# Stick-breaking attention summed by parts over differences of the values, with scans that take two keys a step in long rows

## The chip, the core and the metric

The kernel runs on one core of a Trainium2 chip. The metric is the device time of one execution in microseconds, lower is better. Engines are named as in the profile: PE is TensorE's matmul, PEld its weight load, DVE VectorE, ACT ScalarE, POOL GpSimd, SP SyncE. Each engine works through its own list of instructions in order, and waits where an instruction needs another engine or a transfer.

## The reference

One step of a two-layer streaming encoder: 1024 prompt frames and 8 sample streams of 16 frames, width 1024. Layer 0 has eight stick-breaking heads of width 64 beside a convolution; layer 1 is a band attention; each layer ends with an MLP of width 4096. The change lies in the stick-breaking heads:

```python
def stick_breaking(q, k, v, q_pos, k_pos):
    z = jnp.einsum('bqhd,bkhd->bhqk', q, k).astype(jnp.float32) * (HEAD_DIM ** -0.5)
    mask = k_pos[None, :] < q_pos[:, None]
    log_keep = jnp.where(mask, jax.nn.log_sigmoid(-z), 0.0)
    between = lax.cumsum(log_keep, axis=3, reverse=True) - log_keep
    w = jnp.where(mask, jnp.exp(jax.nn.log_sigmoid(z) + between), 0.0)
    return jnp.einsum('bhqk,bkhd->bqhd', w.astype(v.dtype), v)
```

With keep_j = sigmoid(-z_j), and 1 for a masked key, and S_j the product of keep over the keys from j to the row's end, the weight of key j is sigmoid(z_j) S_{j+1}, which equals S_{j+1} - S_j.

## The kernel before, in words

Everything is kept transposed, with channels on the 128 partitions and tokens along the free axis. The heads of layer 0 are worked on in four pairs p = 0 to 3, in `mixer0`. While a pair's attention runs, other work is laid between its steps: the q, k and v projections of the next pair (`proj`, tiles `sq`, `sk`, `sv`, PSUM tiles `psp`), the two gated inputs of the convolution (`ag`, tiles `u`), the 31 taps of the convolution (`tap`, line 735, two DVE instructions each, tiles `y`), the sample streams (`sample_steps`), and in the last pair the layer norm of the convolution (`conv_norm`) and the first part of the output projection (`part_out`, tiles `psoa`, which read `cat`, loaded through `cr` by `ready_chunks`).

`attend` makes eight jobs a pair: head i = 0 or 1, and t = 0 to 3, two rows of queries each. A row q is 128 queries against n = (q + 1) * 128 keys, so n runs from 128 to 1024. `one(q)` makes the scores in banks of up to 512 keys (lines 924, 925, 927, tile `z`; the last adds a mask of -1e30 on the block of the diagonal). ACT takes sigmoid(z) into `w` (tile `sg`, line 928) and sigmoid(-z) into `keep` (tile `kp`, line 929). `stick` lets DVE turn `keep` into running products from the row's end (a scan along the free axis, line 907: it steps backward through the row, its second input is a constant 1) and multiplies `w` by the product of the keys behind it (line 909). The sample streams do the same with one row of 1152 keys for each of two groups of four streams (`soft`, tiles `sgs` and `kps`).

`weigh_steps` then transposes the weights in blocks of 128 by 128 on PE (`turn`, line 388, PSUM tile `tpa`), copies them to SBUF on ACT (line 390, `wa`), and multiplies them with the values (`prod`, line 398, tile `ava`: two halves of the PSUM bank hold two partial sums). `finish` copies one half with ACT (line 406), adds the halves on DVE (line 410, `cpa`) and stores them. Values reach that product through `expand_v`: PE transposes `sv` in blocks (line 898, `vt`), ACT copies them into `vs` (line 900).

The order of the work is written with numbers: `merge` puts the lists of steps together by their estimated PE times and by lags behind named steps, `level` lays the taps between them by estimated DVE times, and the framework's own scheduler then fixes the order of each engine's list from the dependences. `tap` is recorded after the last DVE instruction of `finish`. Tiles of one tag share buffers: three for `sg`, two for `kp`, one for `sv`.

The pair's `sv` is also an output: POOL issues its store (line 881) when all three parts have been evacuated.

Of the kernel before, what the change touches and what calls it, by code (L numbers as in the profile page):

```python
# [124 lines left out]
def tile_trunk(ctx, tc, ins, outs):  # L125
# [17 lines left out]
    def bank(name):  # L143
        return psum.tile([P, 512], F32, tag="ps", name=name)
# [225 lines left out]
                split(hi, lo, piece[rows, at - c0:at - c0 + m])  # L370
                at += m

    def weigh_steps(vs, wk, cat, i, t, blocks, name, scored):


        order = sorted(blocks.keys, key=lambda j: -len(blocks.keys[j]))
        groups = []
        for two in zip(order[::2], order[1::2]):
            n, m = (P * len(blocks.keys[j]) for j in two)
            groups.append(([(two[0], 0, n), (two[1], n, m)], n + m))  # L380
        st = {"w": {}}

        def turn(gi):
            items, used = groups[gi]
            tp = bank(f"tp{name}{gi}")
            for j, c0, n in items:
                for q, tile_q in enumerate(blocks.keys[j]):
                    nc.tensor.transpose(tp[:, c0 + q * P:c0 + (q + 1) * P], blocks.get(j, tile_q), ident)
            st["w"][gi] = wk.tile([P, 512], F32, tag="wt", name=f"w{name}{gi}")
            ACT(st["w"][gi][:, :used], tp[:, :used], AF.Copy)  # L390

        def prod(gi):

            if gi == 0:
                st["av"] = bank(f"av{name}")
            for m, (j, c0, n) in enumerate(groups[gi][0]):
                o0 = 0 if 2 * t in blocks.keys[j] else P
                mm(st["av"][64 * m:64 * m + 64, o0:o0 + n], vs[:, j, i], st["w"][gi][:, c0:c0 + n], start=gi == 0,
                   stop=gi == last)

        def finish():
            own = slice(64 * i, 64 * i + 64)
            av = st["av"]
            one = P if t == 0 else 0
            tmp = wk.tile([P, 256], F32, tag="av", name=f"at{name}")
            ACT(tmp[own, one:], av[64:128, one:256], AF.Copy)
# [3 lines left out]
            prior["weights"] = tt(piece[own, one:], av[0:64, one:256], tmp[own, one:], ALU.add)  # L410
# [244 lines left out]
    def mixer0():  # L655
        with ExitStack() as st:
# [8 lines left out]
            pp = Bufs(st.enter_context(pool("pair0")))  # L665
            wk = Bufs(st.enter_context(pool("work0")), wt=4, wts=1, cat=2)
            S = {"qb": qb}

# [216 lines left out]
            def expand_qk(p):  # L885
# [19 lines left out]
            def stick(w, keep, n):  # L905

                nc.vector.tensor_tensor_scan(keep[:, 0:n][:, ::-1], keep[:, 0:n][:, ::-1],  # L907
                                             ones[:, 0:1].to_broadcast([P, n]), 1.0, ALU.mult, ALU.mult)
                tt(w[:, 0:n - 1], w[:, 0:n - 1], keep[:, 1:n], ALU.mult)

            def attend(p, cat):
                def job(i, t):
                    ws = {}

                    def one(q):
                        n = (q + 1) * P
                        w = ep.tile([P, TP], F32, "sg", f"sg{p}{i}{q}")
                        keep = ep.tile([P, TP + P], F32, "kp", f"kp{p}{i}{q}")
                        qc = slice(q * P, q * P + P)
                        for c in range(0, n, 512):  # L920
                            m = min(512, n - c)
# [3 lines left out]
                            mm(z[:, :m], qs[i][:, qc], kl[i][:, c:c + m], start=False, stop=not last)  # L925
                            if last:
                                mm(z[:, m - P:m], unit, maskd, start=False, stop=True)
                            ACT(w[:, c:c + m], z[:, :m], AF.Sigmoid)
                            ACT(keep[:, c:c + m], z[:, :m], AF.Sigmoid, scale=-1.0)
                        stick(w, keep, n)  # L930
                        ws[q] = w
# [8 lines left out]
                    def dcost(q):  # L940
# [2 lines left out]
                    name = f"a{p}{i}{t}"  # L943
                    return (Step(cost(q0), lambda: one(q0), dcost(q0)),
                            Step(cost(q1), lambda: one(q1), dcost(q1), f"z{name}"),
                            weigh_steps(vs, wk, cat, i, t, blocks, name, f"z{name}"))

                return [job(i, t) for i in range(2) for t in range(4)]

            def soft(bg, z, zn, s):  # L950
# [1016 lines left out]
```

## Time and profile before

| what | us |
|---|---|
| median of 3 runs (lowest, highest) | 2755.19 (2753.42, 2755.53) |
| span of the profiled execution, first to last instruction | 2748.2 |
| what the median has beyond that span | 7.0 |
| busy: PE, DVE, ACT, POOL | 2669.0, 2090.5, 1389.0, 328.3 |
| mean granted TensorE clock | 0.991 |

The profiled execution's own time is its span; only the 7.0 us between it and the median of the runs are not seen in the trace. In the profile, "idle before" is the time in which an engine stood still before an instruction, and what is named behind an arrow is what ended it. A matmul's busy time overlaps with the next one's, so a busy PE needn't be PE at its peak. PEclk is the granted share of TensorE's clock. Times in a row of the timeline are the start, counted from the span's first instruction, and the length of a run of like instructions.

### The profile page before, as it was taken

What the parts mean: (1) busy time and instruction counts of PE and PEld (TensorE: products, weight loads), DVE (VectorE), ACT (ScalarE), POOL (GpSimd) and SP (SyncE); (2) the same over time, 40 slices, a digit from 0 to 9 for tenths busy, and PEclk for the clock granted to TensorE, in tenths of its full rate; (3) what the DMA queues carried; (4) which work ended last, traced back from release to release, by engine and by line L of the source; (5) the groups of instructions that cost most, each with busy time, mean ns of one, the idle gap of its engine ahead of it and who ended that gap; (6) DMA issues with size and microseconds to landing.
All of it is one profiled execution on the core that took longest, in us unless ns stands there. A gap on an engine that the chain in (4) does not pass through costs nothing.

```text
span 2748.2 us, 50583 instructions
## 1 busy us (share of the span) xinstructions
PE 2669.0 (97%) x19362; PEld 2557.1 (93%) x19362; DVE 2090.5 (76%) x4117; ACT 1389.0 (51%) x2906; POOL 328.3 (12%) x599
## 2 busy tenths in 40 slices
PE   8999898999999999999999999998999999999998
PEld 8987776799999999999999999997999999999998
DVE  8999998888777755758577777778787777647577
ACT  5344456755554543435355555556555555434344
POOL 1100101041111100000011111110221111100001
PEclk9999999999999999999999999999999999999999
DMA  4434446454343377435444444446533343684344
GB/s 157 121 111 147 118 141 223 145 176 143 139 146 141 138 260 250 124 100 170 146 140 138 140 135 135 139 132 229 179 132 137 141 145 138 230 270 134 96 125 145
DMA packets 173203, 422.90 MB, mean 154 GB/s; under 512 B 25968, under 2 KB 53808, under 8 KB 170912
## 3 DMA queue, kind: packets, MB, share of 16 engines
q1 hardware_dynamic: 135696, 288.38, 33.1%
q0 software_dynamic: 37120, 131.27, 13.9%
q8 instruction: 152, 2.49, 0.4%
q14 instruction: 91, 0.75, 0.1%
q10 hardware_dynamic: 144, 0.02, 0.0%
HBM read 289.60 MB, written 117.34 MB: 148 GB/s over the span
## 4 chain that ended last, share of the span: by engine, by line
PE 76%; DVE 12%; ACT 4%; issue 4%; DMA 3%; POOL 0%; SPq 0%; DVEq 0%; ACTq 0%; POOLq 0%
PE um L1461 25%; PE pd L1686 25%; PE psc L225 10%; PE psp L225 3%; DVE y L735 3%; PE avc L467 2%; PE tpc L455 2%; DVE kp L907 2%; PE f L225 1%; PE psoa L225 1%; DMA cr<-cat_d 1%; PE zc L1201 1%; PE zc L1202 1%; PE zs L568 1%; PE so L602 1%
## 5 line engine op out<-in xcount | busy, mean ns | idle before, releaser
L225 PE MATMUL psc<-h,hl_wc 128*128 128x384 f32 x1728 | 327.2, 339 | 0.0
L225 PEld LDWEIGHTS psc<-h,hl_wc 128*128 128x128 f32 x1728 | 296.8, 188 | 13.3 <-issue 10.9
L1461 PE MATMUL um<-sl,hl_m 128*128 128x288 f32 x1548 | 240.3, 295 | 0.0
L1461 PEld LDWEIGHTS um<-sl,hl_m 128*128 128x128 f32 x1548 | 217.7, 188 | 0.0
L1686 PE MATMUL pd<-tm,hl_wd 128*128 128x288 f32 x1584 | 214.7, 294 | 0.0
L1686 PEld LDWEIGHTS pd<-tm,hl_wd 128*128 128x128 f32 x1584 | 211.3, 189 | 0.0
L735 DVE SCALAR_TENSOR_TENSOR y<-u,dw,y 128x1024 f32<-128x1024 f32 (+1 forms) x232 | 177.8, 806 | 0.6
L225 PE MATMUL psp<-h,hl_wi 128*128 128x384 f32 x864 | 165.7, 344 | 0.0
L1468 ACT ACTIVATE hdm<-hdm 128x288 f32<-128x288 f32 x192 | 84.7, 442 | 156.5 <-DVE hdm L1467 154.8
L225 PEld LDWEIGHTS psp<-h,hl_wi 128*128 128x128 f32 x864 | 150.9, 191 | 7.0 <-issue 6.2
L186 DVE TENSOR_TENSOR tm<-xr,tm 128x576 fp32r<-128x576 f32 (+1 forms) x120 | 85.8, 715 | 93.9 <-ACT tm L185 93.6
L185 ACT ACTIVATE tm<-xr 128x576 fp32r<-128x576 f32 (+1 forms) x120 | 77.6, 646 | 95.8 <-PE pd L1686 74.0
L1168 ACT ACTIVATE s<-s,mxc 128x640 f32<-128x640 f32 (+4 forms) x128 | 88.9, 694 | 60.2 <-DVE mxc L1165 58.6
L1461 PE MATMUL um<-sl,hl 128*128 128x288 f32 x756 | 119.1, 296 | 0.0
L1686 PE MATMUL pd<-th,hl_wd 128*128 128x288 f32 x792 | 113.7, 297 | 3.8 <-DVE th L186 3.7
L1686 PEld LDWEIGHTS pd<-th,hl_wd 128*128 128x128 f32 x792 | 108.2, 190 | 4.8 <-DVE th L186 4.2
L1686 PE MATMUL pd<-xr,hl_wd 128*128 128x288 f32 x792 | 112.4, 296 | 0.0
L1686 PEld LDWEIGHTS pd<-xr,hl_wd 128*128 128x128 f32 x792 | 108.0, 190 | 0.0
L1461 PEld LDWEIGHTS um<-sl,hl 128*128 128x128 f32 x756 | 106.4, 188 | 0.8
L1686 PE MATMUL pd<-tm,hl 128*128 128x288 f32 x768 | 104.9, 295 | 0.0
L1686 PEld LDWEIGHTS pd<-tm,hl 128*128 128x128 f32 x768 | 103.1, 188 | 0.0
L185 ACT ACTIVATE whc<-tpc 128x512 fp32r<-128x512 f32 (+1 forms) x144 | 72.5, 523 | 46.7 <-PE tpc L455 45.8
(526 smaller groups left out, 6637.0 us busy)
## 6 DMA issues: line engine op xcount, KB each, us to landing
xr<-hb_d SPq DMA_DIRECT2D x208, 288.0 KB, 3.0
xr<-in_w_up_dram SPq DMA_DIRECT2D x64, 512.0 KB, 4.2
hb_d<-hdm POOLq DMA_DIRECT2D x96, 288.0 KB, 2.4
hb_d<-t POOLq DMA_DIRECT2D x96, 288.0 KB, 2.4
wm<-in_w_down_dram SPq DMA_DIRECT2D x64, 256.0 KB, 4.0
st_wd<-in_w_down_dram SPq DMA_DIRECT2D x64, 256.0 KB, 3.5
st_wc<-in_w_in_c_dram SPq DMA_DIRECT2D x44, 256.0 KB, 2.9
xm_d<-xo POOLq DMA_DIRECT2D x16, 576.0 KB, 3.5
```

The source lines that it names most:

```text
L185: ACT(hi, src, AF.Copy)
L186: return tt(lo, src, f(hi), ALU.subtract)
L225: mm(ps()[:, :G], hl[:, a, at:at + P], act[g][k // 4][b][:, k % 4, :], start=n == 0, stop=n == len(todo) - 1)
L455: nc.tensor.transpose(tp[:, c0 + q * P:c0 + (q + 1) * P], blocks.get(j, tile_q), ident)
L467: mm(st["av"][:, o0:o0 + n], vs[:, j, i].rearrange("p a d -> p (a d)"), src[:, c0:c0 + n], start=st["done"] == 0, stop=st["done"] == nmm - 1)
L568: mm(box["z"][at // 512][own, at % 512:at % 512 + kw], qb[:, own], k[:, b * kw:b * kw + kw], start=True, stop=True)
L735: stt(src if j == CW - 1 else dst, src, wj, dst, ALU.mult, ALU.add)
L907: nc.vector.tensor_tensor_scan(keep[:, 0:n][:, ::-1], keep[:, 0:n][:, ::-1], ones[:, 0:1].to_broadcast([P, n]), 1.0, ALU.mult, ALU.mult)
L1168: ACT(s[:, :n], s[:, :n], AF.Exp, bias=mx, scale=-1.0, accum_out=tot)
L1461: mm(banks[b, n][:, :TQ], w[:, a, c * P:c * P + P], combo(key, c)[:, h, n * TQ:n * TQ + TQ], start=k < 3 and c == 0 and i == 0, stop=c == ...
L1468: ACT(y, y, AF.Relu)
L1686: mm(ps, w[:, a, m * P:m * P + P], b[:, h, (n - ns[0]) * TQ:(n - ns[0]) * TQ + TQ], start=first and s == 0, stop=j == NJ - 1 and s == 2, s ...
```

## The change

Summed by parts, the sum over a row's n keys of (S_{j+1} - S_j) v_j is v_{n-1} plus the sum over j of S_j (v_{j-1} - v_j), with v_{-1} = 0. So the product on PE can take the running products S as they are, if the values are replaced by differences of neighbours, and if the last value of the row's end is added to each output column.

- `one(q)` no longer makes sigmoid(z) (line 928 before) and no longer multiplies by it (line 909 before). One tile, with the tag `sg`, holds `keep` and then S.
- `stick` scans rows under 512 keys as before. In rows of 512 keys and more the scan steps over pairs: it reads the odd keys and the even keys, multiplies both into the running product, and writes S at the even keys (n/2 steps, each input and the output with a step of two elements). A product of n/2 - 1 elements, again with a step of two, makes the odd keys' S.
- `differences(p)`, new, runs ahead of a pair's first transposes of values: four ACT copies of 64 x 8 take the value at the end of each block of 128 keys into `ve`; one DVE subtraction of 128 x 1023 turns `sv` into differences in place, stepping backward; one ACT instruction of 128 x 1 negates the first column. The subtraction overwrites `sv`, so it waits for the store of `sv`; the transposes wait for it.
- `finish` adds the row ends: instead of one ACT copy of 64 x 256 there are two ACT instructions of 64 x 128, each with its own column of `ve` as bias. Where t = 0 there were two instructions before, and are two now.
- `soft` keeps both sigmoids and the product of 1151 elements; its scan of 1152 becomes a scan of 576 and a product of 575.

```diff
@@ finish
-            ACT(tmp[own, one:], av[64:128, one:256], AF.Copy)
...
-            if one:
-                ACT(piece[own, :one], av[0:64, :one], AF.Copy)
+            for e in range(2):
+                cols = slice(e * P, e * P + P)
+                dst, rows = (piece, slice(0, 64)) if one and e == 0 else (tmp, slice(64, 128))
+                ACT(dst[own, cols], av[rows, cols], AF.Identity, bias=ends()[rows, i, 2 * t + e:2 * t + e + 1])
@@ mixer0
+            def differences(p):
+                v = S["sv", p]
+                ends = S["ends", p] = pp.tile([P, 2, 8], F32, "ve", f"ve{p}")
+                for i in range(2):
+                    for rows in (slice(0, 64), slice(64, 128)):
+                        ACT(ends[rows, i], v[64 * i:64 * i + 64, P - 1:TP:P], AF.Copy)
+                tt(v[:, 1:TP][:, ::-1], v[:, 0:TP - 1][:, ::-1], v[:, 1:TP][:, ::-1], ALU.subtract)
+                ACT(v[:, 0:1], v[:, 0:1], AF.Copy, scale=-1.0)
@@ expand_v
+                if g == 0:
+                    differences(p)
@@ stick
-                nc.vector.tensor_tensor_scan(keep[:, 0:n][:, ::-1], keep[:, 0:n][:, ::-1],
-                                             ones[:, 0:1].to_broadcast([P, n]), 1.0, ALU.mult, ALU.mult)
-                tt(w[:, 0:n - 1], w[:, 0:n - 1], keep[:, 1:n], ALU.mult)
+                if n < 512:
+                    nc.vector.tensor_tensor_scan(keep[:, 0:n][:, ::-1], keep[:, 0:n][:, ::-1],
+                                                 ones[:, 0:1].to_broadcast([P, n]), 1.0, ALU.mult, ALU.mult)
+                    return
+                even, odd = keep[:, 0:n:2], keep[:, 1:n:2]
+                nc.vector.tensor_tensor_scan(even[:, ::-1], odd[:, ::-1], even[:, ::-1], 1.0, ALU.mult, ALU.mult)
+                tt(odd[:, :n // 2 - 1], odd[:, :n // 2 - 1], even[:, 1:], ALU.mult)
@@ one(q)
-                        w = ep.tile([P, TP], F32, "sg", f"sg{p}{i}{q}")
-                        keep = ep.tile([P, TP + P], F32, "kp", f"kp{p}{i}{q}")
+                        keep = ep.tile([P, TP], F32, "sg", f"sg{p}{i}{q}")
...
-                            ACT(w[:, c:c + m], z[:, :m], AF.Sigmoid)
                             ACT(keep[:, c:c + m], z[:, :m], AF.Sigmoid, scale=-1.0)
@@ soft
-                stick(w, keep, TP + P)
+                stick(keep, TP + P)
+                tt(w[:, 0:TP + P - 1], w[:, 0:TP + P - 1], keep[:, 1:TP + P], ALU.mult)
```

Where the lists of instructions differ matters at three places. In the rows below, a name's number tells its tile, and a scan is listed as SCALAR_TENSOR_TENSOR; line numbers of the changed kernel are up to 19 higher.

The first is PE's list at the start of pair 0, where the transposes of the values (`vt`, from `sv`) stand among the projections of pair 1 (`psp`); `z` are scores, `zs` a sample stream's scores. Before, they stand in the middle of a projection of 24 matmuls:

```order
L225 MATMUL psp_1108<-h_31_172,hl_wi_0_966 128x384
L225 MATMUL psp_1108<-h_30_171,hl_wi_0_966 128x384
L898 MATMUL vt_1121<-ident,sv_1003 128x128 x3
L898 MATMUL vt_1128<-ident,sv_1003 128x128 x3
L898 MATMUL vt_1133<-ident,sv_1003 128x128 x3
L568 MATMUL zs_1140<-ct00k_1142,qb_124 32x256 x4
L225 MATMUL psp_1108<-h_40_178,hl_wi_1_971 128x384
```

Now they stand behind the whole of it:

```order
L225 MATMUL psp_1105<-h_71_191,hl_wi_1_971 128x384
L225 MATMUL psp_1105<-h_70_190,hl_wi_1_971 128x384
L913 MATMUL vt_1125<-ident,sv_1003 128x128 x3
L913 MATMUL vt_1132<-ident,sv_1003 128x128 x3
L913 MATMUL vt_1137<-ident,sv_1003 128x128 x3
L570 MATMUL zs_1144<-ct00k_1146,qb_124 32x256 x4
L943 MATMUL z_1173<-k_743,q_741 128x256
```

The transposes moved back by twelve matmuls; what they wait for on DVE is new.

The second is DVE's list at the same time. `y` and `u` are taps, `hl_wi` are weights split for PE, `sq` is an evacuation. Before:

```order
L186 TENSOR_TENSOR hl_wi_1_1093<-st_wi_1_1091,hl_wi_1_1093 128x512
L907 SCALAR_TENSOR_TENSOR kp_1099<-kp_1099,ones 128x128
L735 SCALAR_TENSOR_TENSOR y_771<-u_382,dw,y_771 128x1024
L909 TENSOR_TENSOR sg_1098<-sg_1098,kp_1099 128x127
L735 SCALAR_TENSOR_TENSOR y_771<-u_382,dw,y_771 128x1024
L735 SCALAR_TENSOR_TENSOR y_771<-u_382,dw,y_771 128x128
```

Now:

```order
L186 TENSOR_TENSOR hl_wi_1_1093<-st_wi_1_1091,hl_wi_1_1093 128x512
L923 SCALAR_TENSOR_TENSOR sg_1098<-sg_1098,ones 128x128
L737 SCALAR_TENSOR_TENSOR y_771<-u_382,dw,y_771 128x1024
L737 SCALAR_TENSOR_TENSOR y_771<-u_382,dw,y_771 128x128
L737 SCALAR_TENSOR_TENSOR y_771<-u_382,dw,y_771 128x1024
L903 TENSOR_TENSOR sv_1003<-sv_1003 128x1023
```

The subtraction came in behind three taps, and the product of 127 left.

The third is DVE's list where the last row of pair 0 ends (head 1), at its row of 1024 keys; `l` and `q` (lines 351, 353) prepare the next pair's keys and queries. Before:

```order
L877 TENSOR_TENSOR sv_2101<-psp_2110,rh_315 128x384
L735 SCALAR_TENSOR_TENSOR y_1239<-u_389,dw,y_1239 128x128
L735 SCALAR_TENSOR_TENSOR u_389<-u_389,dw,y_1239 128x1024
L735 SCALAR_TENSOR_TENSOR u_389<-u_389,dw,y_1239 128x8x16
L351 TENSOR_TENSOR l_745<-sk_1870,k_743 64x1024
L907 SCALAR_TENSOR_TENSOR kp_2126<-kp_2126,ones 128x1024
L351 TENSOR_TENSOR l_746<-sk_1870,k_744 64x1024
L909 TENSOR_TENSOR sg_2125<-sg_2125,kp_2126 128x1023
```

Now:

```order
L879 TENSOR_TENSOR sv_2071<-psp_2080,rh_315 128x384
L737 SCALAR_TENSOR_TENSOR y_1237<-u_389,dw,y_1237 128x128
L737 SCALAR_TENSOR_TENSOR u_389<-u_389,dw,y_1237 128x1024
L928 SCALAR_TENSOR_TENSOR sg_2095<-sg_2095 128x512
L737 SCALAR_TENSOR_TENSOR u_389<-u_389,dw,y_1237 128x8x16
L929 TENSOR_TENSOR sg_2095<-sg_2095 128x511
L351 TENSOR_TENSOR l_746<-sk_1848,k_744 64x1024
```

The scan and its product now stand ahead of the preparation of the next pair.

More of the change, by code (lines that the diff above doesn't have):

```diff
@@ L371, in put, with weigh_steps @@
                 at += m
-    def weigh_steps(vs, wk, cat, i, t, blocks, name, scored):
+    def weigh_steps(vs, ends, wk, cat, i, t, blocks, name, scored):
         order = sorted(blocks.keys, key=lambda j: -len(blocks.keys[j]))
@@ L903, in expand_v, with stick @@
                     ACT(S["vn"], tp[:, 2 * P:3 * P], AF.Copy)
-            def stick(w, keep, n):
-                nc.vector.tensor_tensor_scan(keep[:, 0:n][:, ::-1], keep[:, 0:n][:, ::-1],
-                                             ones[:, 0:1].to_broadcast([P, n]), 1.0, ALU.mult, ALU.mult)
-                tt(w[:, 0:n - 1], w[:, 0:n - 1], keep[:, 1:n], ALU.mult)
+            def stick(keep, n):
+                if n < 512:
[5 more added lines that the diff above has]
+                tt(odd[:, :n // 2 - 1], odd[:, :n // 2 - 1], even[:, 1:], ALU.mult)
             def attend(p, cat):
@@ L927, in one @@
                                 mm(z[:, m - P:m], unit, maskd, start=False, stop=True)
-                            ACT(w[:, c:c + m], z[:, :m], AF.Sigmoid)
                             ACT(keep[:, c:c + m], z[:, :m], AF.Sigmoid, scale=-1.0)
-                        stick(w, keep, n)
-                        ws[q] = w
+                        stick(keep, n)
+                        ws[q] = keep
                     keys = {j: [q for q in (2 * t, 2 * t + 1) if j <= q] for j in range(2 * t + 2)}
@@ L945, in job @@
                             Step(cost(q1), lambda: one(q1), dcost(q1), f"z{name}"),
-                            weigh_steps(vs, wk, cat, i, t, blocks, name, f"z{name}"))
+                            weigh_steps(vs, lambda: S["ends", p], wk, cat, i, t, blocks, name, f"z{name}"))
                 return [job(i, t) for i in range(2) for t in range(4)]
```

2 lines of the change are left out of this document (1 added, 1 removed).

## The prediction

> **What bounds the kernel now.** I read the page first, for the whole.
>
> ```profile
> span 2748.2 us, 50583 instructions
> PE 2669.0 (97%) x19362; PEld 2557.1 (93%) x19362; DVE 2090.5 (76%) x4117; ACT 1389.0 (51%) x2906; POOL 328.3 (12%) x599
> ```
>
> PE is busy nearly all the time, so a change on DVE or ACT can only bring back time in which PE stands still. The changed instructions lie between 105 us (first scores) and 547 us (last addition of halves), so the second view is the busy time by windows of that stage (PE, PEld, DVE, ACT, POOL, each with its count; then PEclk and DMA).
>
> ```profile
> 105.00:205.00 100.00, 97.86 (x721) 85.55 (x723) 97.67 (x131) 49.65 (x116) 8.47 (x15) 1.00 0.43 128
> ...
> 315.00:415.00 100.00, 93.24 (x717) 77.76 (x716) 98.68 (x127) 53.31 (x127) 10.61 (x19) 0.98 0.48 148
> 415.00:547.00 132.00, 117.61 (x853) 92.38 (x852) 112.06 (x201) 98.59 (x213) 16.07 (x29) 0.96 0.57 190
> sum 442.00, PE 408.35 PEld 340.74 DVE 414.21 ACT 249.84 POOL 44.66; mean PE 102.09 PEld 85.19 DVE 103.55 ACT 62.46 POOL 11.17
> ```
>
> Unlike in the whole kernel, DVE is here as full as PE: 414.2 of 442 us, 98 to 99% in the first window and the third. PE stands still for 442 - 408.35 = 33.7 us, the most that waits alone can give back. PE's list of waits in the same window says on whom (total, times, longest).
>
> ```profile
> PE tpa L388 <- DVE sg L909: 20.2, 8, 6.2
> PE psoa L225 <- ACT cat L185: 5.0, 3, 2.6
> PE sn L582 <- DVE cpa L410: 1.2, 1, 1.2
> ...
> PE tpa L388 <- DVE xo L1086: 0.4, 1, 0.4
> ```
>
> The transposes of the weights wait 20.2 us for the product that the change removes; seven smaller waits for DVE, the first and last of which are shown, make 5.5 us more. The rest is ACT's. The longest wait, at the end of pair 0, shows how it arises.
>
> ```profile
> 206.02 4.44 PE L225 MATMUL psp<-h,hl_wi 128*128 128x384 f32 x24
> ...
> 211.15 0.54 DVE L877 TENSOR_TENSOR sv<-psp,rh 128x384 f32<-128x384 f32 x1
> 211.62 0.33 DVE L735 SCALAR_TENSOR_TENSOR y<-u,dw,y 128x128 f32<-128x128 f32 x1
> 211.88 1.53 DVE L735 SCALAR_TENSOR_TENSOR u<-u,dw,y 128x1024 f32<-128x1024 f32 x2
> 213.34 1.21 DVE L351 TENSOR_TENSOR l<-sk,k 64x1024 fp32r<-64x1024 f32 x1
> 214.47 2.27 DVE L907 TENSOR_TENSOR_SCAN kp<-kp,ones 128x1024 f32<-128x1024 f32 x1
> 218.03 1.23 DVE L909 TENSOR_TENSOR sg<-sg,kp 128x1023 f32<-128x1023 f32 x1
> 211.94 0.33 PE L388 MATMUL tpa<-ident,sg 128*128 128x128 f32 x1
> 219.31 0.90 PE L388 MATMUL tpa<-ident,sg 128*128 128x128 f32 x3 [6.17 <-DVE sg L909]
> ```
>
> DVE works through its list without a gap and is simply late: a backlog, not a missing input.
>
> **The change part by part.** DVE first. These rows give its costs (busy, mean ns).
>
> ```profile
> L907 DVE TENSOR_TENSOR_SCAN kp<-kp,ones 128x1024 f32<-128x1024 f32 x8 | 18.3, 2284 | 0.2
> L907 DVE TENSOR_TENSOR_SCAN kp<-kp,ones 128x128 f32<-128x128 f32 x8 | 3.3, 412 | 0.0
> L909 DVE TENSOR_TENSOR sg<-sg,kp 128x127 f32<-128x127 f32 (+3 forms) x64 | 47.9, 749 | 0.6
> L909 DVE TENSOR_TENSOR sg<-sg,kp 128x1023 f32<-128x1023 f32 x8 | 9.8, 1219 | 0.2
> L909 DVE TENSOR_TENSOR sg<-sg,kp 128x127 f32<-128x127 f32 x8 | 2.2, 280 | 0.0
> ```
>
> A scan of m steps costs 145 + 2.09 m ns by its first two rows, a product 145 + 1.05 m by its last two. Eight heads have rows of 512, 640, 768, 896 and 1024 keys, 3840 in all. Removed: their scans, 8 x (5 x 145 + 2.09 x 3840) = 70.0 us; all products by sigmoid(z), 47.9; the samples' scans of 1152, 8 x 2.55 = 20.4; together 138.3. Added: scans of half the steps, 8 x (725 + 2.09 x 1920) = 37.9; products for the odd keys, 8 x (725 + 1.05 x 1915) = 21.9; for the samples 8 x (1.35 + 0.75) = 16.8; four subtractions of 1023 at 1.22, 4.9; together 81.5. DVE loses 57 us of 414, 14 a pair.
>
> No row shows DVE with a step of two elements. Two bounds: as a step of one (the numbers above), or twice the time per element, since a scan already needs twice a product's (2.09 against 1.05). A gain is excluded, as each element still has to be processed. Doubling the products alone adds 8 x (1.05 x 1915 + 1.05 x 575) = 20.9 us, doubling the scans too another 8 x (2.09 x 1920 + 2.09 x 576) = 41.7. I take the step of one, the row of the same instruction on the same type, and keep both others as rivals.
>
> ACT loses line 928 and gains little:
>
> ```profile
> L928 ACT ACTIVATE sg<-z 128x512 f32<-128x512 f32 (+2 forms) x96 | 47.8, 498 | 19.8 <-PE z L927 10.1 <-PE tpa L388 4.6 <-PE z L925 4.1
> L406 ACT ACTIVATE ata<-ava 64x128 f32<-64x128 f32 x8 | 2.2, 274 | 8.5 <-PE ava L398 8.4
> ```
>
> Its twenty small instructions for `ve` and the first column are at most 274 ns each, 5.5 us, and 24 split copies add under 274 each, 6.6: net 36 us less on an engine at 57% here. Costed at nothing, but it helps: each row's scan can start one sigmoid earlier.
>
> What it brings. With 14 us less a pair, DVE's 97.7 us in the first window become 84, below PE's 97.9: the backlog goes and PE sets the pace. At 219.31 the wait is then set by the inputs. `sv` is ready when its matmuls end, the first twelve of the 24 at 206.02, so about 208.3; behind it stand the tap rows, 0.33 + 1.2, the scan of 512, 1.2, the small tap, 0.3, and the product, 0.7: done by 212.6, where PE comes at 212.05. So 0.5 of 6.2 stays. The next longest (4.1, below) stands at the end of pair 2 and shrinks the same way; for the six others I leave 1.0 in all. Gain 20.2 - 1.5 = 18.7. Of the other 5.5 I take half, 2.7, since those instructions also wait for PE.
>
> TensorE's clock adds to it:
>
> ```profile
> 306.79 0.97 PE L388 MATMUL tpa<-ident,sg 128*128 128x128 f32 x6 [1.64 <-DVE sg L909]
> ...
> 215.20:222.00 6.80, 2.69 (x10) 2.69 (x11) 6.63 (x9) 0.60 (x1) 2.91 (x7) 0.50 0.84 212
> 307.40:310.80 3.40, 3.40 (x40) 2.70 (x38) 3.34 (x5) 0.92 (x2) 0.53 (x1) 0.50 0.19 25
> 406.40:409.80 3.40, 3.40 (x13) 3.30 (x12) 3.34 (x5) 2.21 (x6) 0.54 (x1) 0.50 0.12 31
> ...
> sum 23.80, PE 16.86 PEld 14.05 DVE 19.18 ACT 10.60 POOL 8.15; mean PE 3.37 PEld 2.81 DVE 3.84 ACT 2.12 POOL 1.63
> ```
>
> The last row sums five stretches in which the granted clock was 0.50. The three shown lie at or just behind waits for line 909, as the row above shows for the second; PE worked 2.69 + 3.40 + 3.40 = 9.5 us in them, and would do it in half. Gain 4.7.
>
> What it costs. At the start of pair 0 the transposes of values now wait for a subtraction.
>
> ```profile
> 106.27 2.34 PE L225 MATMUL psp<-h,hl_wi 128*128 128x384 f32 x12
> 106.97 0.56 POOL L881 DMA_DIRECT2D out_sb_v_dram<-sv  x1 [3.93 <-ACT sv L879]
> DMA to landing us min/median/max: 4.0/4.0/4.0
> 109.32 1.25 DVE L735 SCALAR_TENSOR_TENSOR y<-u,dw,y 128x1024 f32<-128x1024 f32 x1
> ```
>
> The store lands at 106.97 + 4.0 = 111.0. On DVE the taps from 109.32 take 1.25 + 0.3 + 1.25, so the subtraction runs from 112.1 to 113.3, not held by the store; ACT's one column, 0.3, ends at 113.6. PE has 24 matmuls from 106.27, twice some 2.2 us, and is there at 110.6: a new wait of 3.0 us. Without the twelve matmuls that moved ahead it would be 5.2. Queued behind ACT's column are the copies of `vs` and the next row's sigmoids, which wait for PE anyway. In pairs 1 to 3 `sv` is made in the pair before, so that store and subtraction have time; I take ACT's one column, 0.3 each, 0.9. A half-clock stretch of 3.4 us behind the new wait costs 1.7, at even odds 0.9. The Trainium skill (TensorE: Matmul & The Clock Gate, What's actually happening) puts the half clock behind an idle window of about 3.4 us; here it also followed a wait of 1.64 us, at 307.4, so I don't count the 3.0 as safe.
>
> At the end of pair 2 a part of the gain comes back:
>
> ```profile
> 419.08 1.05 ACT L348 ACTIVATE k<-sk 64x1024 fp32r<-64x1024 f32 x1 [0.17 <-PE z L924]
> ...
> 424.81 0.34 SPq L1062 DMA_DIRECT2D cr<-cat_d  x1
> 429.67 1.03 PE L388 MATMUL tpa<-ident,sg 128*128 128x128 f32 x6 [4.14 <-DVE sg L909]
> 432.69 1.35 ACT L185 ACTIVATE cat<-cr 128x384 fp32r<-128x384 f32 x3 [1.84 <-DMA cr<-cat_d]
> 433.27 0.69 PE L225 MATMUL psoa<-cat,hl_wo0a 128*128 128x384 f32 x1 [2.57 <-ACT cat L185]
> ```
>
> The load of `cr` starts when DVE has read `sk` (line 351), and lands 7.9 us later. DVE's line 351 waits for ACT's copy of k, at 419.08 + 1.05, and takes 1.2, so the load can start at 421.4, 3.4 us sooner: of 4.1 us 0.8 turn into a wait for `cat`.
>
> Sum: -18.7 - 2.7 - 4.7 + 3.0 + 0.9 + 0.9 + 0.8 = -20.5. Span 2727.7, and with the 7.0 us around it 2734.7.
>
> **The rivals.** A measurement of this kernel tells 0.2%, 5.5 us, from no change.
>
> Strided products cost double. The Trainium skill speaks for it (Vector Engine (DVE) Microarchitecture Reference, Measured stream behaviour on trn2): a port keeps its full rate only on runs of at least two adjacent 4-byte words, and a two-source operation whose elements stand apart took 1.73 to 2.51 ns a column instead of 1.05. Against it the same skill (Advanced Engine Details and Errata, SBUF Cachelines) asks for two hits on a 16-byte line, which a step of 8 bytes has. No run here shows either. DVE then saves 57 - 21 = 36 us and stays at 378 of 442. I take half of the waits and of the clock: 10.1 + 1.4 + 2.4 - 5.6 = 8.3 gained, 2747. Chance 0.22.
>
> The waits change owner. PE's list already has ACT and a load behind DVE; if the ends of pairs stay bound by loads and by ACT's order, only the six short waits go, 20.2 - 6.2 - 4.1 = 9.9, less the 5.6 of costs: 2751, no change that can be told. For it speaks the row at 433.27, against it that ACT is half idle. Chance 0.10.
>
> Slower: scans and products both double. DVE gets 20.9 + 41.7 - 57 = 6 us more, in a stage where it is at 96 to 99% and PE already waits for it; with the 3.0, 0.9 and 0.9 of new costs the time is 2755.2 + 11 = 2766. It decides from the point where an element at a step of two costs about 1.9 times as much in both. Against it: a scan spends 2.09 ns on an element, in which a slower port could hide. Chance 0.08.
>
> **How the numbers follow.** The forecast has 0.60. All DVE waits and half of the 16.9 us of busy PE in half-clock stretches gone, at 2 us of cost, would be about 2723; the rivals of 2747 and 2751 set the upper end at 2752. Faster: 0.60 x 0.98 + 0.22 x 0.9 + 0.10 x 0.2 = 0.81. Slower 0.08, the rest 0.11.
>
> **What would show it.** Right: DVE near 357 us busy over the stage, scans of 512 at 1.2 us and products of 511 at 0.7, waits of `tpa` under 5 us, one wait of some 3 us of `vt` for ACT or DVE in pair 0. Wrong: products of 511 near 1.3 us (first rival), long new waits of PE for `cat`, `vs` or loads (second), scans of 512 near 2.3 us (third), or a stage still 440 us long with DVE at 80%, which would mean that PE's own rate sets it.

## The result and the profile after

| kernel | median, us | runs | lowest to highest |
|---|---|---|---|
| before, same session | 2754.3 | 4 | 2749.0 to 2755.5 |
| changed | 2729.8 | 4 | 2726.0 to 2730.9 |

The ratio is 0.9914, 95% interval 0.9900 to 0.9928: about 24 us less. The forecast was 2734.7 us. The changed kernel was timed once more in a later set: 2728.6 us, ratio 0.9912 (0.9894 to 0.9930).

The page's first lines, for the whole kernel:

```profile
span 2728.9 us, 50505 instructions
PE 2662.6 (98%) x19362; PEld 2553.8 (94%) x19362; DVE 2040.6 (75%) x4105; ACT 1365.7 (50%) x2854; POOL 330.5 (12%) x599
```

The matmuls are the same 19362. DVE has lost 50 us, and the span is 19.3 us shorter than before's 2748.2. The windows of the stage, as in the prediction (PE, PEld, DVE, ACT, POOL with counts, then PEclk and DMA); by the count of matmuls the stage now ends at 527 instead of 547 us:

```profile
205.00:315.00 110.00, 109.99 (x823) 95.56 (x822) 103.90 (x156) 48.84 (x117) 13.22 (x22) 1.00 0.45 140
...
415.00:527.00 112.00, 105.51 (x763) 83.00 (x762) 85.05 (x180) 82.47 (x178) 9.06 (x17) 0.98 0.56 189
sum 422.00, PE 404.49 PEld 340.07 DVE 365.66 ACT 228.10 POOL 45.37; mean PE 101.12 PEld 85.02 DVE 91.41 ACT 57.02 POOL 11.34
```

The row to look at is the first: PE is busy 109.99 of 110 us there, at full clock. In that window PE alone sets the pace. Over the stage it stands still for 422 - 404.49 = 17.5 us, against 33.7 before. PE's waits in the same window:

```profile
PE psoa L225 <- ACT cat L185: 8.0, 3, 5.7
PE vt L913 <- ACT sv L904: 2.9, 1, 2.9
PE tpa L388 <- DVE sg L929: 2.2, 2, 1.3
PE zs L570 <- ACT qb L561: 1.3, 1, 1.3
...
```

The 20.2 us behind line 909 have become 2.2 us behind line 929, two short waits. The other waits for DVE shrank from 5.5 to about 1.4 us. Two owners are new or bigger: `cat` (5.0 before, 8.0 now) and `vt` (none before, 2.9 now). The place that had the longest wait before, the end of pair 0, now reads:

```profile
210.48 0.55 PE L388 MATMUL tpa<-ident,sg 128*128 128x128 f32 x3
210.78 4.42 PE L225 MATMUL psp<-h,hl_wi 128*128 128x384 f32 x24
211.21 0.55 DVE L879 TENSOR_TENSOR sv<-psp,rh 128x384 f32<-128x384 f32 x1
...
213.13 1.21 DVE L928 TENSOR_TENSOR_SCAN sg<-sg 128x512 f32<-128x512 f32 x1
214.27 0.32 DVE L737 SCALAR_TENSOR_TENSOR u<-u,dw,y 128x128 f32<-128x128 f32 x1
214.51 0.68 DVE L929 TENSOR_TENSOR sg<-sg 128x511 f32<-128x511 f32 x1
...
216.67 0.66 PE L388 MATMUL tpa<-ident,sg 128*128 128x128 f32 x4
```

The product of the last row ends at 215.19 and the 24 matmuls at 215.20. PE comes to the row's transposes at 216.67, behind a few other matmuls: DVE is done 1.5 us ahead of it, and 6.2 us of waiting are 0. The durations by form, of the instructions that the change adds:

```profile
L928 DVE TENSOR_TENSOR_SCAN sg<-sg 128x512 f32<-128x512 f32 x8 | 9.7, 1217 | 2.1 <-ACT sg L947 2.0
L929 DVE TENSOR_TENSOR sg<-sg 128x511 f32<-128x511 f32 x8 | 5.5, 691 | 0.2
L928 DVE TENSOR_TENSOR_SCAN sg<-sg 128x256 f32<-128x256 f32 x8 | 5.4, 678 | 1.0 <-ACT sg L947 1.0
L923 DVE TENSOR_TENSOR_SCAN sg<-sg,ones 128x256 f32<-128x256 f32 x8 | 5.5, 684 | 4.4 <-ACT sg L947 4.4
L411 ACT ACTIVATE ata<-ava,ve 64x128 f32<-64x128 f32 x56 | 17.8, 358 | 27.9 <-PE ava L398 27.5
```

Row two answers the first rival, which had 1.3 us for a product of 511: it takes 691 ns. The scans answer the third, which had 2.3 us for a scan of 512: it takes 1217 ns, and a scan of 256 steps takes 678 ns with a step of two words (line 928) and 684 ns with a step of one (line 923). The step of two costs nothing.

### The profile page after: what moved, and what is told of

Read it like the earlier page. It is cut to its first block, busy times and chain, and to the rows that moved or that the text cites. A ratio compares the mean times of both kernels' runs of the same rounds, so it can differ in the third digit from the quotient of the medians.

```text
span 2728.9 us, 50505 instructions
## 1 busy us (share of the span) xinstructions
PE 2662.6 (98%) x19362; PEld 2553.8 (94%) x19362; DVE 2040.6 (75%) x4105; ACT 1365.7 (50%) x2854; POOL 330.5 (12%) x599
## 4 chain that ended last, share of the span: by engine, by line
PE 84%; DVE 7%; ACT 3%; issue 3%; DMA 3%; POOL 0%; SPq 0%; DVEq 0%; ACTq 0%; POOLq 0%
PE pd L1705 26%; PE um L1480 25%; PE psc L225 10%; PE psp L225 4%; PE avc L469 2%; PE tpc L457 2%; PE psoa L225 2%; PE f L225 1%; PE zs L570 1%; PE zc L1220 1%; PE ava L398 1%; DVE y L737 1%; PE so L604 1%; PE psg L225 1%; PE psa L225 1%
```

## The experiments

The theory: DVE's backlog in the stage is what PE waited for, and taking 57 us from DVE brings the gain. Its rivals: the gain is ACT's, which has lost half of its sigmoids; or it is the latency of the longest rows' scans alone. Ratios are to the kernel before, run on the same chip in the same set.

### DVE's load put back

```diff
                         stick(keep, n)
+                        extra = ep.tile([P, TP + P], F32, "kp", f"kp{p}{i}{q}")
+                        tt(extra[:, 0:n - 1], keep[:, 0:n - 1], keep[:, 1:n], ALU.mult)
```

> The changed kernel, and behind each row's scan one more product of n-1 elements into a spare tile that nobody reads: 64 products, in the mean 575 elements, 145 + 1.05 x 575 = 749 ns each by the prediction's own line, 48 us in all, which puts VectorE's stage back from 366 to about 414 us, where it was before (414). ScalarE keeps its saving. Theory (the gain comes from VectorE's backlog, which TensorE's transposes of the weights wait for): the waits of tpa for sg return, though not in full, since a useless product delays only what is behind it in VectorE's queue and a row's own transposes may start ahead of it; 12 to 20 us of tpa waits in the stage, 2742 to 2752 us. Rival (the gain comes from ScalarE's 47 us fewer sigmoids, or from the shorter scan alone, VectorE's load being beside the point): tpa waits below 6 us, at most 2734 us.

2746.0 us, ratio 0.9980 (0.9970 to 0.9990). The added products take 47.8 us (64 of 747 ns in the mean), and 18 of the 24 us are gone. The stage is 440 us long again, with DVE at 402.7 (414 were expected: 47.8 us is a sum of rows, and busy time counts what overlaps once). PE stands still for 440 - 406.91 = 33.1 us of it, as long as before the change (33.7). Its windows, the second one around the longest new wait, and PE's waits:

```profile
104.00:544.00 440.00, 406.91 (x3006) 340.78 (x3006) 402.67 (x653) 228.00 (x520) 44.89 (x80) 0.97 0.48 150
222.00:236.00 14.00, 8.08 (x50) 6.46 (x49) 13.94 (x21) 3.16 (x8) 0.54 (x1) 0.76 0.40 130
```

```profile
PE vt L913 <- ACT sv L904: 10.5, 3, 5.9
PE psoa L225 <- ACT cat L185: 9.2, 2, 5.8
PE tpa L388 <- DVE sg L929: 7.0, 4, 3.3
```

The time is as the theory had it, the place isn't: I had expected 12 to 20 us at `tpa`, and only 7.0 stand there (2.2 without the added products). More, 10.5 us in three waits (2.9 without them), stands at `vt`, so in pairs 1 and 2 too. Their subtraction queues behind DVE's backlog like any other instruction:

```profile
230.96 1.20 DVE L903 TENSOR_TENSOR sv<-sv 128x1023 f32<-128x1023 f32 x1
232.19 0.20 ACT L904 ACTIVATE sv<-sv 128x1 f32<-128x1 f32 x1 [4.51 <-DVE sv L903]
232.45 0.90 PE L913 MATMUL vt<-ident,sv 128*128 128x128 f32 x3 [5.92 <-ACT sv L904]
```

DVE is busy 13.94 of 14 us around it, and PE waits 5.92 us. ACT's saving was untouched in this kernel, and so was each row's own scan: the load alone, placed behind the row, takes three quarters of the gain back.

### ACT's load put back

```diff
+                            ACT(extra[:, c:c + m], z[:, :m], AF.Sigmoid)
                             ACT(keep[:, c:c + m], z[:, :m], AF.Sigmoid, scale=-1.0)
```

> The changed kernel, and ahead of each bank's sigmoid of -z a useless sigmoid of z into a spare tile, as the kernel before had it for the weights: ScalarE's stage goes from 228 to about 275 us, VectorE's stays at 366. Theory (VectorE's backlog): ScalarE has room, each row's scan starts up to 0.75 us later but VectorE is behind at most of these places, so 2730 to 2735 us. Rival (the gain is ScalarE's): most of the 24 us goes, 2745 us or more.

2735.0 us, ratio 0.9940 (0.9926 to 0.9955). ACT is back at 265 us over the stage, and seven tenths of the gain stay. By ratio it is 0.26 to 0.28% slower than the changed kernel, some 7 us, but its interval touches those of the two sets of the changed kernel (0.9928 and 0.9930 at their upper ends), so its size is uncertain. No wait accounts for it: PE stands still for 17.0 us between 100 and 530 us, against 17.5 and 15.4 in the two profiles of the changed kernel. The clock would: the half-clock stretches of the stage sum to 27.3 us, against 13.6 and 17.1. PE worked 20.9 us in them, against 9.8 and 12.1, and half of that difference is 4.4 to 5.5 us. So a minor part, three tenths at most, is ACT's. Even that isn't shown: these are single executions, and where the half-clock stretches fall changes from one to the next (below).

### One part of the change alone

Parts only: every scan of the pairs, the sample streams' too, takes one key a step.

```diff
-                if n < 512:
+                if n < 4096:
```

> The changed kernel with one key a step in every scan of the four pairs, so only the summing by parts is left of the change: a row of 1024 keys costs one scan of 145 + 2.09 x 1024 = 2.29 us in place of 1.22 + 0.69 = 1.91, and of 512 keys 1.22 in place of 0.68 + 0.41; VectorE's stage gets about 14 us more than the 366 of the changed kernel. Theory (the gain goes by VectorE's load; 48 of its 62 us come from the product that the parts do away with): three quarters or more of the gain stays, 2731 to 2737 us. Rival (it goes by the latency of the long scans, which the transposes of the longest rows wait for): half the gain or more goes, 2742 us or more.

2730.6 us, ratio 0.9928 (0.9914 to 0.9943), just under the 2731 to 2737 us that I had expected.

Two keys a step only: the kernel before, with `stick` of the changed kernel ahead of its product by `w`.

> The kernel before with only the two-key scans of long rows; the weights are still made by a sigmoid and a product. VectorE's stage falls by about 14 us from 414 to 400. Theory (load): about 14 of 62 parts of the gain, 2746 to 2752 us, tpa waits of the 20 us down to 12 to 17. Rival (latency of the long scans): half the gain or more, 2742 us or less.

2740.0 us, ratio 0.9964 (0.9951 to 0.9977). I had expected 2746 to 2752 us; the time is the rival's, 2742 or less. Of PE's waits at `tpa`, this row is left of the 20.2 us:

```profile
PE tpa L388 <- DVE sg L914: 13.8, 8, 4.2
```

By ratios the parts alone bring 0.72%, the two keys alone 0.36%, both 0.86%. The two parts add up to 0.22% more than the whole, which is no more than these intervals leave open (some 0.24%). PE's idle time shows it more clearly, in one execution each: between its 500th matmul and its 3560th, PE stands still for 33.8 us before, 21.8 with the two keys alone, 18.7 with the parts alone, and 17.5 and 15.4 in two profiles of both. So the gain saturates: the first 14 us taken from DVE bring 12 us of PE's idle time, the last 14 bring 1 to 3. I had split the gain in proportion to the load, 14 of 62; that was wrong. The rival was nearer with its number, but its reason, the latency of the long scans, doesn't hold: the parts alone leave those scans at one key a step and keep five sixths of the gain. While PE waits at the end of a pair, most of what is taken off the backlog is won; the 20.2 us at `tpa` fell by 6.4, the longest of 6.2 us to 4.2. When DVE has caught up, more brings little.

### The step of two, measured by itself

The changed kernel, with three rounds of instructions of 144 elements behind its start that nobody reads: products at steps of 1, 2, 3, 4, 6, 8 words (lines 988 to 993) and scans at steps of 1, 2, 4, 8 (lines 994 to 997).

```diff
+            def stepped(s):
+                return probe[:, 0:M * s:s]
+            for _ in range(3):
+                tt(stepped(1), stepped(1), stepped(1), ALU.mult)
...
+                nc.vector.tensor_tensor_scan(stepped(8), stepped(8), stepped(8), 1.0, ALU.mult, ALU.mult)
```

> The changed kernel, and behind its start three rounds of products and scans of 144 elements that nobody reads, with steps of 1, 2, 3, 4, 6 and 8 words (scans 1, 2, 4 and 8): only VectorE's durations are read. By the lines 145 + 1.05 m and 145 + 2.09 m ns a product is 296 ns and a scan 446 ns at step 1. If a step costs nothing at step 2 because two words still lie in each 16 bytes, a step of 3 or 4 and more makes the product longer; if steps never cost, all are 296 and 446 within 5 ns; a scan at 2.09 ns an element may hide a slower port up to twice the product's 1.05.

```profile
L988 DVE TENSOR_TENSOR probe<-probe 128x144 f32<-128x144 f32 x3 | 0.9, 295 | 0.0
L989 DVE TENSOR_TENSOR probe<-probe 128x144 f32<-128x144 f32 x3 | 0.9, 295 | 0.0
L990 DVE TENSOR_TENSOR probe<-probe 128x144 f32<-128x144 f32 x3 | 1.0, 346 | 0.0
L991 DVE TENSOR_TENSOR probe<-probe 128x144 f32<-128x144 f32 x3 | 1.2, 407 | 0.0
L993 DVE TENSOR_TENSOR probe<-probe 128x144 f32<-128x144 f32 x3 | 1.4, 469 | 0.0
L994 DVE TENSOR_TENSOR_SCAN probe<-probe 128x144 f32<-128x144 f32 x3 | 1.3, 442 | 0.0
L997 DVE TENSOR_TENSOR_SCAN probe<-probe 128x144 f32<-128x144 f32 x3 | 1.4, 452 | 0.0
```

A product costs 295 ns at a step of 1 and of 2, 346 at 3, 407 at 4, 430 at 6 (not shown) and 469 at 8. A scan costs 442 to 452 at all four steps. Of the two rules of the Trainium skill that the prediction weighed, the cache-line one (Advanced Engine Details and Errata, SBUF Cachelines: two hits on a line of 16 bytes) fits these rows: a step of two words has two in each line, a step of four has one. Why a step of eight costs more than one of four, it does not say. The rule of at least two adjacent words (Vector Engine (DVE) Microarchitecture Reference, Measured stream behaviour on trn2) does not hold for a step of two; its slower rates begin here at a step of three. All three streams of an instruction step alike here. The third rival's ground is gone too: at a step of 8 a scan is still within 10 ns, so its 2.09 ns an element does hide the slower access.

### The two new waits

The first load of `cr` at the end of pair 2, in a buffer of its own:

```diff
-                    fill = ready_chunks(0, range(2), pp, cat_t) + first + [late] + fill
+                    fill = ready_chunks(0, [0], Lent(ep, "kp", T), cat_t) + ready_chunks(0, [1], pp, cat_t) + first + [late] + fill
```

> The changed kernel; at the end of pair 2 the first load of cr (the chunk that the first part of mixer 0's output projection reads) goes into a buffer of its own and need not wait for the one before it. Theory (the 5.7 us that psoa waits for cat there are the late load, and the half-clock stretch from 411.6 to 418.4 us follows from that idle time): the wait falls below 1 us, the stretch goes, 5 to 8 us less, 2722 to 2726 us. Rival (the load is late because the data that it reads back were written late): the wait stays above 4 us and the time at 2728 to 2732.

2724.1 us, ratio 0.9896 (0.9881 to 0.9911). The wait didn't fall below 1 us but from 5.73 to 2.91, now at the load of the next chunk. PE no longer waits for the first chunk; these are the rows of the next:

```profile
398.77 0.34 SPq L1081 DMA_DIRECT2D cr<-cat_d  x1
...
407.76 1.35 ACT L185 ACTIVATE cat<-cr 128x384 fp32r<-128x384 f32 x3 [3.15 <-DMA cr<-cat_d]
408.34 1.33 PE L225 MATMUL psoa<-cat,hl_wo0a 128*128 128x384 f32 x3 [2.91 <-ACT cat L185]
```

The half-clock stretch of 6.8 us did not go either, it begins at 407.7. The time is in the range that I gave, but not by what I gave for it: the longest wait lost 2.8 us instead of 5. All waits of `psoa` for `cat` sum to 2.9 us, against 8.0 and 5.6 in the two profiles of the changed kernel, and PE's idle time between 100 and 530 us is 11.7 us, against 17.5 and 15.4. The same edit on the kernel before:

> The kernel before with only the first load of cr at the end of pair 2 in a buffer of its own. Theory (the wait for cat at that place is small in the kernel before, 2.57 us, because TensorE has just waited 4.1 us for the weights; it grew to 5.73 as that wait went): at most 3 us less than the kernel before, 2747 to 2751 us, ratio 0.999 to 1.000. Rival (the late load costs the kernel before as much as the changed one): 5 us less or more, ratio 0.998 or lower.

2750.6 us, ratio 0.9994 (0.9984 to 1.0005), no difference that can be told. But this doesn't show that the late load cost the kernel before nothing. The buffer has the tag `kp`, which in the kernel before still holds the rows' `keep`, so it isn't the load's own: the load starts at 423.01, when line 909 has just read a `kp` tile, instead of at 424.81. In the changed kernel the same edit let it start at 355.05. In the profile the wait at `tpa` at that place falls from 4.14 to 0.20 us, and `psoa` waits for `cat` twice, 2.7 and 2.2 us. What a really early load would bring to the kernel before stays open.

The transposes of the values later in pair 0:

```diff
+                values = [Step(327.0, lambda p=p, g=g: expand_v(p, g)) for g in range(NG)]
+                if p == 0:
+                    values[0].after, values[0].lag = "za000", 3500.0
...
-                steps += [jobs[0][1]] + body
+                steps += [jobs[0][1]] + ([] if p else values) + body
```

> The changed kernel; in pair 0 alone the transposes of the differences of the values stand behind the second row's scores instead of ahead of them, so that the subtraction on VectorE and ScalarE's one column have more time. Theory (vt's wait of 2.9 us and the half-clock stretch from 114.6 to 121.4 us behind it are what the differences cost): the wait falls below 0.8 us, the stretch goes, 3 to 6 us less, 2724 to 2727 us. Rival (the slack at pair 0's start is taken up by the next wait, as VectorE runs behind there anyway): 2728 to 2731 us with other waits of about 3 us in its place.

2724.0 us, ratio 0.9895 (0.9880 to 0.9909). The wait of `vt` is 2.05 us instead of 2.88, so the edit bought 0.8, not 2; the stretch behind it did go. The 2.05 us lie in two slots of the clock's grid (below), 0.9 and 1.2, so that may be chance. The medians of these two kernels are no higher than the lowest of the nine runs of the changed kernel (2724.1, on another chip), but the intervals of their ratios overlap with its own.

Both edits, and the differences in a tile of their own, so that the subtraction needn't wait for the store:

```diff
-                tt(v[:, 1:TP][:, ::-1], v[:, 0:TP - 1][:, ::-1], v[:, 1:TP][:, ::-1], ALU.subtract)
+                d = S["sd", p] = ep.tile([P, TP + P], F32, "kp", f"sd{p}")
+                tt(d[:, 1:TP], v[:, 0:TP - 1], v[:, 1:TP], ALU.subtract)
```

> Both edits together (cr's first load in a buffer of its own, the transposes of the differences later in pair 0), and the differences written to a tile of their own, so that the subtraction doesn't wait until the values are stored. Theory: the two waits and their half-clock stretches lie at different places and add up, 9 to 13 us less than the changed kernel, 2717 to 2721 us. Rival (later waits take up what is won): at most 4 us less, 2726 us or more.

2716.7 us, ratio 0.9875 (0.9855 to 0.9894), the best version: its four runs, 2715.9 to 2723.4, all lie below the lowest of nine of the changed kernel, 2724.1. The interval stands clear of the changed kernel's first one (from 0.9900) and touches its second (from 0.9894). Its stage takes 408.4 us:

```profile
105.00:513.40 408.40, 397.64 (x3007) 333.70 (x3005) 361.50 (x589) 226.78 (x520) 45.47 (x80) 1.00 0.51 162
```

No half-clock stretch is left in the stage (PEclk 1.00); PE stands still for 408.4 - 397.64 = 10.8 us of it, the wait of `vt` is 0.9 and the longest for `cat` 2.6. By the ratios this kernel is 10 to 11 us below the changed one; its profiled span is 13.6 us below the first one of that. PE's idle time accounts for 17.5 - 10.8 = 6.7 us of the 13.6, the clock for half of the 9.8 us that PE worked in half-clock stretches there (below), 4.9: together 11.6.

### The changed kernel once more

> The changed kernel unaltered, timed once more in five rounds, for the comparison with the three kernels that alter its edges (2724.1, 2724.0 and 2716.7 us). If those gains are real, 2727 to 2732 us and a ratio to the kernel before of 0.990 to 0.993; if the chip of those runs was merely the quicker one, 2724 us and 0.9895. In the profile the wait of vt in pair 0 stands at 2.9 us again; whether a half-clock stretch follows it is even odds, as two of the five other profiles with that wait show none.

2728.6 us (2724.1 to 2732.1), ratio 0.9912 (0.9894 to 0.9930). Its profiled execution took 5.6 us less than the first one's span, 2723.3, with the same waits of `vt` (2.88), `tpa` (2.2) and `psoa` (5.31 the longest). Nearly all of the difference had arisen by the 600th matmul, where it is 5.1 us ahead; 3.7 of it came before the stage begins. The wait of `vt` is the same in both, the clock behind it isn't. Six profiles have that wait at 2.8 to 2.9 us; the granted clock of the 17 us from 108 to 125 is 0.80 twice, 0.90 twice, and 1.00 twice. That is a loss of 3.4, 1.7 or 0 us behind the same wait.

What differs is where the wait lies. In each of the twelve traces all changes of the clock lie on one grid of 3.413 us, within 4 ns over the whole span, and the grid lies elsewhere in each execution. These are two slots of it in the changed kernel's first profile (PEclk is the third figure from the right):

```profile
111.19:114.60 3.41, 1.30 (x8) 0.97 (x6) 3.41 (x5) 0.00 (x0) 0.00 (x0) 1.00 0.56 209
114.60:118.01 3.41, 2.64 (x17) 1.98 (x17) 3.25 (x4) 1.63 (x5) 0.00 (x0) 0.50 0.00 0
```

And two in the kernel with the early `cr` load, whose pair 0 is the same:

```profile
107.31:110.72 3.41, 2.03 (x12) 1.71 (x10) 3.41 (x6) 0.00 (x0) 0.00 (x0) 1.00 0.82 279
110.72:114.13 3.41, 1.91 (x19) 1.37 (x20) 3.41 (x4) 1.52 (x5) 0.00 (x0) 1.00 0.00 0
```

In the first, PE stands still for 3.41 - 1.30 = 2.1 us of one slot, and the next slot runs at half clock. In the second the same wait is split over two slots, 1.4 and 1.5 us, and the clock stays. Of the six profiles, the four with a half-clock stretch have 2.1 to 2.7 us of idle time in one slot, the two without have 1.5 at most. Between 100 and 547 us, in all twelve, each of the 25 slots at full clock with 1.9 us of idle time or more is followed by half clock; with 1.5 to 1.9 us it is 8 of 17, with less 5 of 1467.

## Why the prediction was right, point by point

**The bound.** Right. DVE's load was what PE waited for: taking it away brought the gain, and putting 48 us back behind the rows took 18 of 24 us of it, and brought all of PE's idle time back.

**DVE's saving.** Right: 57 us were predicted, and the rows sum to 165.5 us before (lines 907 and 909) and 108.8 after (lines 903, 923, 928, 929, 976), 56.7 less. Busy time over the stage fell by 48.5 only (414.2 to 365.7, not to 357): the rows of the stage sum to 444 and 390 us, so neighbouring instructions overlap by some 30 and 24 us, which busy time counts once. A saving summed from rows is larger than what the busy time shows.

**The step of two.** Right, at the full rate; the rivals of 2747 and 2766 us were both built on the other price.

**ACT.** Its net saving by rows is 40 us (36 predicted). The split copies take 358 ns each, not "under 274": the row that I had bounded them by is a plain copy without a bias. It didn't matter, since the 256-wide copies that they replace are gone. That the lighter ACT "helps" is right by some 7 us at most, most of which the clock of one execution would explain; the prediction counted nothing for it.

**The waits.** `tpa` gave 18.0 (18.7 predicted), the other waits for DVE some 4 (2.7). Of the 2.2 us left at `tpa`, 1.3 stand at the end of pair 2, where lines 351 and 353 still come ahead of the last row's scan on DVE. In pair 0 `vt` waits 2.88 us (3.0 predicted), from 112.49 to 115.37:

```profile
113.78 1.21 DVE L903 TENSOR_TENSOR sv<-sv 128x1023 f32<-128x1023 f32 x1
115.03 0.20 ACT L904 ACTIVATE sv<-sv 128x1 f32<-128x1 f32 x1 [5.06 <-DVE sv L903]
115.37 2.15 PE L913 MATMUL vt<-ident,sv 128*128 128x128 f32 x9 [2.88 <-ACT sv L904]
```

The chain is the predicted one. Both ends are some 1.8 us later than forecast, since this execution comes to the 24 matmuls ahead of it 1.8 us later (108.07 against 106.27). In pairs 1 to 3 PE doesn't wait for `vt` at all (0.9 predicted).

**The wait for `cat`.** Mis-sized. "Of 4.1 us 0.8 turn into a wait for `cat`"; it grew by 3.2, from 2.57 to 5.73:

```profile
400.96 1.05 ACT L348 ACTIVATE k<-sk 64x1024 fp32r<-64x1024 f32 x1 [0.17 <-PE z L943]
...
403.38 1.22 DVE L351 TENSOR_TENSOR l<-sk,k 64x1024 fp32r<-64x1024 f32 x1
404.62 0.34 SPq L1081 DMA_DIRECT2D cr<-cat_d  x1
407.89 0.98 PE L388 MATMUL tpa<-ident,sg 128*128 128x128 f32 x7 [1.29 <-DVE sg L929]
414.03 1.35 ACT L185 ACTIVATE cat<-cr 128x384 fp32r<-128x384 f32 x3 [4.47 <-DMA cr<-cat_d]
414.60 0.69 PE L225 MATMUL psoa<-cat,hl_wo0a 128*128 128x384 f32 x1 [5.73 <-ACT cat L185]
```

The load does start when line 351 ends (404.60), as the step said. But line 351 does not start when ACT's copy of k ends, as the step had it. That copy ends at 402.01, and line 351 stands behind taps on DVE until 403.38, 1.37 us; before the change it was 3.43 (420.13 to 423.56). Counted from the end of the copy, the load starts 2.07 us sooner than before, not 3.4. PE is through with its transposes at 408.87, where it had been at 430.70: 3.71 us sooner counted from the copy, not 4.1. And from its start until it is read the load takes 9.41 us instead of 7.88. 3.71 - 2.07 + 1.53 makes the 3.2. The step took DVE's delay ahead of line 351 as gone, and the load's own time as fixed. Why the load takes longer is not shown.

**The clock.** Right in sum. The half-clock stretches in the stage went from 23.8 to 13.6 us, in which PE worked 9.83 us instead of 16.86, half of the difference is 3.5; the prediction had 4.7 - 0.9 = 3.8. The parts are not all the forecast's. The three stretches that it counted are gone; so is the one from 512.2, which it didn't count and in which PE worked 3.14 us, 1.6 more. The one at the end of pair 2 is still there, now at the wait for `cat` (3.80 us of busy PE, 4.23 before). The new one behind `vt` costs 6.03 / 2 = 3.0 us, where 0.9 was counted. That the sum is close is luck. These are the two that the stage has now:

```profile
114.60:121.40 6.80, 6.03 (x32) 3.99 (x33) 4.82 (x7) 3.07 (x8) 0.00 (x0) 0.50 0.24 77
411.60:418.40 6.80, 3.80 (x19) 2.49 (x19) 2.63 (x4) 2.53 (x6) 2.14 (x4) 0.50 1.08 354
```

Even odds of a 3.4-us stretch were too low for the first: four of six profiles have one, of 3.4 us or 6.8, by where the wait lies on the clock's grid.

**The sum and the 7.0 us around it.** The sum was some 3 to 4 us too small. The span fell by 19.3 us in the first profile and by 24.9 in the second (20.5 predicted), but spans also hold what an execution gains or loses outside the stage. From PE's 500th matmul to its 3560th, the kernel before and the changed one:

```profile
100.96:552.13 451.17, 417.40 (x3062) 349.32 (x3061) 421.31 (x612) 252.81 (x577) 45.18 (x81) 0.97 0.48 149
```

```profile
102.76:530.71 427.95, 410.44 (x3062) 346.02 (x3061) 369.63 (x600) 229.16 (x525) 45.88 (x81) 0.98 0.49 157
```

That is 23.2 us less, and 24.6 in the second profile (426.6 us), as the ratios have it. PE's idle time gives 16.3 and 18.4 us of it (16.7 predicted), the clock 3.5 and 2.4 (3.8). The rest, 3.4 and 3.8 us, is a term that the sum did not have: for the same matmuls, PE's busy time less half of what lies at half clock is 405.5 and 405.1 us, where it was 408.9. What shortened it is not shown.

The last term, "with the 7.0 us around it", was off too. In each of the eleven profiled executions since, the run's own time is 1.8 us over its span. If that held before, the profile of before was of an execution of about 2750.0 us, 5 us below the median it was set against, and the 7.0 were 1.8 around the span and 5.2 between executions. The forecast came out 4.9 us too high: 4.0 because the gain is larger, 24.5 us between the medians of the session, and 0.9 because the median of before is lower in that session. With 1.8 the same sum would give 2748.2 - 20.5 + 1.8 = 2729.5 us, where 2729.8 was measured; that would be luck, as the gain in it is too small.

**The rivals.** "The waits change owner" was right in one place: at the end of pair 2 the wait for `cat` took 3.2 us back. The 2.9 us at `vt` were among the forecast's own costs. It wasn't the main thing.

## What to carry to other kernels

Where two engines are nearly level in a stage, read the gain of a lighter one from the other's waits, not from the busy time saved: here the first 14 us off DVE brought 12 us of PE's idle time and the last 14 brought 1 to 3, so two edits that each help needn't add up. When such a wait goes, look at each transfer that was under way during it and compare its landing with the time at which the reader will now be there, not with the time at which it can start, and look for what its engine still does ahead of the instruction that starts it; a second edit that moves it may be worth as much as the next speed-up of the engine. A span and a median are of different executions: take what lies around the span from a run's own time. And a control is one only where its edit does the same thing in both kernels: a buffer that is free in one may be in use in the other.

## What the runs showed of the hardware

- f32 operands with a step of two words run at the full rate on DVE, in products (295 ns for 144 elements, as at a step of one) and in scans (678 ns for 256 steps, 684 at a step of one); a product's element costs 0.78 ns more at a step of four ((407 - 295) / 144) and 1.2 ns more at eight, a scan's nothing up to eight.
- One and the same wait of 2.9 us was followed by 0, 3.4 or 6.8 us at half clock in six executions. The clock changes on a grid of 3.413 us that lies elsewhere in each execution, and what counts is how much of one slot PE stands still: with 1.9 us or more, 25 of 25 slots were followed by half clock. The Trainium skill (TensorE: Matmul & The Clock Gate, What's actually happening) has the clock watched in free-running windows of 3413 ns; the traces agree with that. That only waits of about 3.4 us count is not what they show.
- An ACT copy of 64 x 128 out of PSUM takes 358 ns as `AF.Identity` with a column as bias, 274 as `AF.Copy` without.
